# First gates' sigmoids behind attention's exponentials, early tiles for the third product's weights, and mLSTM heads gated one by one

## The chip, the cores and the metric

The kernel runs on one core of one Trainium2 chip. The metric is the device time of one execution in microseconds (us), lower being better.

## The reference

Two layers of a hybrid decoder on 512 tokens of width 1024, in float32. Each layer computes one wide projection of the normalised input, from it two branches, merges them by gates, and adds a squared-ReLU MLP:

```python
    z = h @ w_in
    q_a, k_a, v_a, q_m, k_m, v_m, o_m, if_m, gates = jnp.split(z, splits, axis=-1)
    ...
    att = sliding_window_attention(q_a, k_a, v_a, att_sinks)
    ...
    hm = mlstm_chunkwise(...)
    hm = rmsnorm(hm, m_head_norm.reshape(M_HEADS, M_V_DIM)).reshape(B, S, M_V_W)
    hm = hm * jax.nn.sigmoid(o_m)

    g_a, g_m = jnp.split(gates, 2, axis=-1)
    mixed = jax.nn.sigmoid(g_a) * (att @ w_att_branch) + jax.nn.sigmoid(g_m) * (hm @ w_m_branch)
    x = x + mixed @ w_out

    u = jax.nn.relu(rmsnorm(x, norm_ffn) @ w_ff1)
    return x + (u * u) @ w_ff2
```

Attention has 8 query heads of 64 in 2 key/value groups, a window of 128 tokens and a learned sink per head that enters the softmax's denominator. The mLSTM branch has 4 heads with values of 128; each head is normalised by itself before the output gate sigmoid(o_m).

## The kernel before

A layer is `mixer` and then `mlp`. The change lies in `mixer`, in the part after the attention's projections.

**Products.** A float32 operand is split into a high and a low part (`wh`, `wl` of a weight, L165 and L166; `split`, L175 and L176, of an activation: the high part is a copy on ACT, the low part a subtraction on DVE), and a product is three TensorE matmuls: high by high, low by high, high by low. A weight chunk is 128x512, loaded on SP's queue (L155); its product with all 512 tokens is 12 matmuls.

**The weave.** The work is issued by `weave(fill, side)`: `fill` is the list of product steps in their order on TensorE, `side` a list of (time, function) pairs that are put in between at their time, counted in chunks of 12 matmuls. A scheduler then orders the instructions of each engine, by priority and by when it expects them to be ready; `tc.high_priority()` lifts what is issued inside it, `tc.issue_after(x)` keeps what is issued inside it behind instruction x. An engine runs its own instructions strictly in the order so made. Tiles come from pools: activations 128x512 from 32 slots (`slot()`, named `a`), temporaries from 17 (`temp()`, named `t`), three PSUM banks (`aux`) for the side work and five (`mm`) for products. A tile that is asked for waits for its buffer's last reader.

The fill after the attention's projections: mLSTM queries and keys; gate A in two halves (`s0`, `s1`, whose results are the four tiles each of `g0` and `g1`); the attention branch product in two halves (`a_steps`), whose results are multiplied into `g0` and `g1` by `ev_a` (L909); seven products that give values and the output gate (`vo_steps`); gate B (`s2`, `s3`).

**Gates.** The evacuation `ev` (L699) multiplies a gate's product by the row norm into a slot; after the last of `g1`, `sigmoid` (L686) is issued for all eight tiles, and `back` (L692) loads the table of Exp and Ln again. Sigmoid lies in another table, so ACT_TABLE_LOAD rows appear around it. Copies run with either table.

**Attention.** Its eight units (b, kv), block b of 128 queries and group kv, are on the side list: scores (L587 to L601), softmax (row maximum L608, its combination with the sinks L609, the sink's term L611, four exponentials L614, the sink's exponential `es` L616, denominators L617 and L618, scaling L619), transposes into PSUM (L52 on TensorE) with a split into high and low (L175, L176) and a causal select of both on POOL (L634), and the output (four matmuls; L645 and L649 bring both halves together, L652 and L653 split the result into tiles `a` for the branch product). The last units are (3,0) and (3,1).

**Values and the output gate.** They come from 2x2 blocks by a scheme of seven products instead of eight, in the order 5, 1, 3, 6, 2, 7, 4. Their weights are sums of blocks of `w_in`: `load` (L714) copies a block on SP's queue, `more` (L718) adds another to it by an accumulating DMA on POOL's. `wa` serves products 5, 6 and 4, and is begun early by `begin` (L727); `wb` serves 3 and 7, and is loaded where product 3 first asks for it, in `weight` (L732). `parts_of` (L723, L724) splits such a weight; products 1 and 2 take plain blocks, as chunks of the ordinary kind. The activations' sums are `sums[n]`. `value` and `output` (L795, L797) evacuate into `vm` and `so`; `gates_o` takes the sigmoid of `so`.

**mLSTM heads.** `m_decay`, `m_weights` and `m_out` (L860 to L892) handle head h and block t; `m_out` leaves its result in `hm[t]`, columns of head h, and the sum of squares in `hss` (L892). `m_norm` (L895 to L901) makes the norms and, for each t, multiplies `hm[t]` by them (L900) and by `so[t]` (L901). `head_tr(f)` transposes head f of all four blocks (L52) for the mLSTM branch product.

Of the kernel before, what the change touches and what calls it, by code (L numbers as in the profile page):

```python
# [9 lines left out]
F32R = mybir.dt.float32r  # L10
# [23 lines left out]
def hybrid_kernel(ctx, tc, x, norm_mix, w_in, att_q_norm, att_k_norm, att_sinks, m_gate_bias,  # L34
# [27 lines left out]
    def nm(s):  # L62
        uid[0] += 1
        return f"{s}_{uid[0]}"
# [323 lines left out]
    def mixer(l, norm, late, order, phase):  # L388
# [152 lines left out]
            gp.tensor_tensor(xv[:, :, 0:ROPE], t1, t2, op=ALU.add)  # L541

        att_acts = [(slot(F32R), slot(F32R)) for _ in range(4)]
        qT, sps, parts = {}, {}, {}
        tri_i = tri_l.bitcast(I32)

        def k_vec(b):
# [55 lines left out]
        def att_softmax(b, kv):  # L603
            sp = sps[b, kv]
            s3 = sp.rearrange("p (h k) -> p h k", h=4)
            hs = slice(4 * kv, 4 * kv + 4)
            m = sm([P, 4], "m")
            ve.tensor_reduce(m, s3, axis=AX.X, op=ALU.max)  # L608
            ve.scalar_tensor_tensor(m, m, -1.0, nsinks[:, l, hs], op0=ALU.mult, op1=ALU.min)  # L609
            es = sm([P, 4], "es")  # L610
            ve.tensor_tensor(es, sinks[:, l, hs], m, op=ALU.add)  # L611
            den = sm([P, 4], "den")
            for i in range(4):
                sc.activation(s3[:, i, :], s3[:, i, :], AF.Exp, bias=m[:, i:i + 1],  # L614
                              accum_out=den[:, i:i + 1])
            sc.activation(es, es, AF.Exp)  # L616
            ve.tensor_tensor(den, den, es, op=ALU.add)  # L617
            ve.reciprocal(den, den)  # L618
            ve.tensor_tensor(s3, s3, den.unsqueeze(2).to_broadcast([P, 4, P]), op=ALU.mult)  # L619
# [90 lines left out]
            return W[(4 * i + k) * P:(4 * i + k + 1) * P, c0:c0 + T]  # L710

        def load(r, i, j, k):
            with tc.high_priority():
                nc.sync.dma_start(r, block(i, j, k))  # L714

        def more(r, i, j, k):
            with tc.high_priority():
# [9 lines left out]
        def begin(k):  # L727
            wa[k] = temp()
            load(wa[k], 0, 0, k)
            more(wa[k], 0, 1, k)  # L730

        def weight(n, k):  # L732
            if n in (1, 2):
                return chunk([block(n - 1, 0, k)])
            if n == 3:
                wb[k] = slot()
                load(wb[k], 1, 1, k)
            w = parts_of((wb if n in (3, 7) else wa)[k])
            if n == 5:
                more(wa[k], 1, 1, k)  # L740
            if n == 6:
                more(wa[k], 1, 0, k)
            if n == 3:
                more(wb[k], 0, 1, k)
            return w
# [2 lines left out]
            return [f32(g[:, :, H * t:H * (t + 1)]) for g in norm.groups[i]]  # L748

        def sum_parts(key, src):  # L750
            sums[key] = [split(src[:, 2 * p:2 * p + 2, :], get=lambda: now["tmp"].tile([P, 2, H], F32R, tag="t", name=nm("t")))
                         for p in range(2)]

        def sums1():
            a, b = (mid.tile([P, 4, H], F32, tag=t, name=nm("sc")) for t in ("mid6", "kvi"))
# [91 lines left out]
        side += [(8.45 + 3.0 * i, f) for i, f in enumerate((gating0, gating1, gating2, gating3))]  # L847
        side += [(9.6 + 1.65 * n, lambda n=n: qk_split(n // 2, n % 2)) for n in range(8)]
        g0, s0 = gate_steps(0)
        g1, s1 = gate_steps(1, lambda: back(sigmoid(g0 + g1)))  # L850

        hm = q_tok
        hss = sm([P, NB, MH], "hss", 1)
# [27 lines left out]
        def m_out(h, t):  # L881
            ps = aux([P, MV + 1])
            for s in range(t + 1):
                pe.matmul(ps, wts[h, s][:, (t - s) * P:(t - s + 1) * P], vm[0][:, s, h, :],
                          start=s == 0, stop=s == t)
            dn = sm([P, 1], "dn")
            ve.scalar_tensor_tensor(dn, ps[:, MV:], -1.0, em[:, t, h:h + 1], op0=ALU.mult, op1=ALU.max)
            ve.tensor_tensor(dn, ps[:, MV:], dn, op=ALU.max)
            ve.reciprocal(dn, dn)
            hs = hm[t][:, h * MV:(h + 1) * MV]  # L890
            sc.activation(hs, ps[:, :MV], AF.Copy, scale=dn)
            sc.activation(ps[:, :MV], hs, AF.Square, accum_out=hss[:, t, h:h + 1])  # L892

        def m_norm():
            ve.tensor_scalar(hss, hss, 1.0 / MV, EPS, op0=ALU.mult, op1=ALU.add)  # L895
            hr = sm([P, NB, MH], "hr", 1)
            rsqrt(hr, hss, "hq")
            for t in range(NB):
                h3 = hm[t].rearrange("p (h v) -> p h v", h=MH)
                ve.tensor_tensor(h3, h3, hr[:, t, :].unsqueeze(2).to_broadcast([P, MH, MV]), op=ALU.mult)  # L900
                ve.tensor_tensor(hm[t], hm[t], so[t], op=ALU.mult)  # L901

        prod = []

# [7 lines left out]
                              ev_a)  # L912

        side += [(25.0 + 0.5 * k, lambda k=k: begin(k)) for k in range(4)]
        side += [(25.0, sums1), (28.5, lambda: sums_next(6, 0, 0)), (31.5, lambda: sums_next(3, 0, 1)), (36.5, sums3)]
        pace = 3.2
        for h in range(MH):
            at = 39.6 + pace * h
            side.append((at, lambda h=h: m_decay(h)))
            for i in range(NB):  # L920
                side += [(at + 1.75 + pace * i / NB, lambda h=h, i=i: m_weights(h, i)),
                         (at + 4.65 + pace * i / NB, lambda h=h, i=i: m_out(h, i))]
        side.append((56.9, m_norm))
        g2, s2 = gate_steps(2)
        g3, s3 = gate_steps(3, lambda: back(sigmoid(g2 + g3)))
# [5 lines left out]
                pe.transpose(ps[:, b * P:(b + 1) * P], hm[b][:, f * P:(f + 1) * P], ident)  # L931
            hmT.append(split(ps, g_head(l, f)))

        side += [(58.4 + 1.0 * f, lambda f=f: head_tr(f)) for f in range(MH)]
        weave(feat_steps(acts, wcols(C_QM, 512), ev_qk) + s0 + s1 + a_steps(0, g0) + a_steps(1, g1) + vo_steps
              + s2 + s3, side)
        sgm = [g2, g3]
# [549 lines left out]
```

## Time and profile before

| | |
|---|---|
| median of 3 runs | 1325.09 us (1323.92 to 1325.39) |
| the profiled execution | 1325.29 us, of which its span is 1323.6 us |
| TensorE busy (PE) | 1290.8 us, 98% of the span, 6930 matmuls |
| VectorE busy (DVE) | 1011.8 us, 76% |
| ScalarE busy (ACT) | 798.0 us, 60% |
| GpSimd busy (POOL) | 227.9 us, 17% |

A line of a timeline gives the start in us from the span's start, the busy time, engine, source line, operation, output <- input tiles, shapes, and how many instructions were joined; in brackets stands the idle time of that engine before it and what ended that. PE is TensorE's matmuls, DVE VectorE, ACT ScalarE, POOL GpSimd, SP SyncE (DMA issues). PEclk is the clock that TensorE was granted, 1 being full speed. Line numbers are those of the kernel before.

### The profile page before, as it was taken

To read this page: it belongs to the slowest core of one execution; us is meant where nothing else is said; L and a number is where in the kernel's file an instruction comes from. 1 tells how busy PE (TensorE), PEld (TensorE's weight loads), DVE (VectorE), ACT (ScalarE), POOL (GpSimd) and SP (SyncE) were. 2 spreads that over 40 slices of the span, in tenths; PEclk is the share of its full clock that TensorE was granted. 3 is DMA by queue.
4 is the path that set the end of the run, shared out by engine and by line. 5 is a ranking of instruction groups with operands and counts; after the bars stand their busy time and mean duration, and the time that the engine had idled before them with its cause. 6 is when DMAs were issued, how large, how long until landed. Compare 5 with 4: busy or idle time off the path is not lost. (4 is left out here: it accounts for less than half of the span.)

```text
span 1323.6 us, 19221 instructions
## 1 busy us (share of the span) xinstructions
PE 1290.8 (98%) x6930; PEld 1097.9 (83%) x6930; DVE 1011.8 (76%) x1581; ACT 798.0 (60%) x1385; POOL 227.9 (17%) x313
## 2 busy tenths in 40 slices
PE   9999799999999999999999988999999999999998
PEld 7877677878889999999888766788888899999987
DVE  4699876576578897978958998665746778879697
ACT  5568568643565665656554784695534656666563
POOL 4511230000003121131115112210000030311310
PEclk9999899999999999999999998999999999999999
DMA  5422483263358989898124225822723698988953
GB/s 152 109 73 64 97 165 89 71 214 121 89 150 154 232 192 204 201 207 220 32 75 111 64 64 115 179 65 72 238 80 97 159 180 233 186 207 201 204 158 96
DMA packets 135150, 186.00 MB, mean 141 GB/s; under 512 B 10376, under 2 KB 78832, under 8 KB 135056
## 3 DMA queue, kind: packets, MB, share of 16 engines
q1 hardware_dynamic: 94208, 131.82, 32.3%
q0 software_dynamic: 40128, 52.57, 25.1%
q8 instruction: 54, 0.88, 0.3%
q10 hardware_dynamic: 720, 0.40, 0.1%
q14 instruction: 40, 0.33, 0.1%
HBM read 182.65 MB, written 2.10 MB: 140 GB/s over the span
## 5 line engine op out<-in xcount | busy, mean ns | idle before, releaser
L47 PE MATMUL mm<-i,wh 128*128 128x512 f32 (+1 forms) x1280 | 355.5, 363 | 0.0
L983 ACT ACTIVATE wh<-raw 128x1024 fp32r<-128x1024 f32 x212 | 223.0, 1055 | 187.4 <-PE mm L47 116.6
L984 DVE TENSOR_TENSOR wl<-raw,wh 128x1024 fp32r<-128x1024 f32 x212 | 255.4, 1221 | 75.0 <-ACT wh L983 75.0
L47 PEld LDWEIGHTS mm<-i,wh 128*128 128x128 f32 x1280 | 223.8, 189 | 31.0 <-DVE a L699 0.8
L47 PE MATMUL mm<-i,wl 128*128 128x512 f32 (+1 forms) x640 | 230.2, 360 | 0.0
L166 DVE TENSOR_TENSOR wl<-w,wh 128x512 fp32r<-128x512 f32 (+1 forms) x192 | 129.2, 676 | 106.9 <-ACT wh L165 103.9
L165 ACT ACTIVATE wh<-w 128x512 fp32r<-128x512 f32 (+1 forms) x192 | 116.9, 610 | 125.3 <-PE mm L47 94.2
L47 PE MATMUL mm<-wh,uh 128*128 128x512 f32 x440 | 171.8, 390 | 0.0
L47 PE MATMUL mm<-wl,uh 128*128 128x512 f32 x440 | 171.7, 390 | 0.0
L47 PE MATMUL mm<-wh,ul 128*128 128x512 f32 x440 | 171.2, 389 | 0.0
L1143 POOL DMA_DIRECT2D raw<-in_w_ff_dram x48 | 62.2, 1303 | 545.7 <-DMA raw<-in_w_ff_dram 370.1
L47 PEld LDWEIGHTS mm<-i,wl 128*128 128x128 f32 x640 | 120.8, 189 | 17.7 <-DVE wl L984 0.4
L47 PE MATMUL mm<-wh,i 128*128 128x512 f32 (+1 forms) x352 | 100.7, 360 | 2.6 <-ACT wh L165 2.3
L1029 DVE SCALAR_TENSOR_TENSOR x<-mm,ms,x 128x512 f32<-128x512 f32 x126 | 90.7, 745 | 9.2 <-PE mm L47 9.1
L47 PEld LDWEIGHTS mm<-wh,ul 128*128 128x128 f32 x440 | 82.6, 188 | 17.6
L47 PEld LDWEIGHTS mm<-wh,uh 128*128 128x128 f32 x440 | 82.8, 188 | 16.0
L47 PEld LDWEIGHTS mm<-wl,uh 128*128 128x128 f32 x440 | 82.8, 188 | 15.5
L47 PE MATMUL mm<-wh,a 128*128 128x512 f32 x256 | 81.8, 393 | 0.0
L47 PE MATMUL mm<-a,wh 128*128 128x512 f32 x256 | 79.3, 391 | 0.0
L47 PEld LDWEIGHTS mm<-wh,i 128*128 128x128 f32 x352 | 61.9, 188 | 14.2 <-ACT wh L165 3.3
L1300 POOL DMA_DIRECT2D raw<-in_w_ff_dram x36 | 44.1, 1224 | 149.4 <-DVE wl L984 100.9
L47 PE MATMUL aux<-i,wh 128*128 128x256 f32 x384 | 69.5, 283 | 0.0
(283 smaller groups left out, 2430.9 us busy)
## 6 DMA issues: line engine op xcount, KB each, us to landing
raw<-in_w_ff_dram SPq DMA_DIRECT2D x144, 512.0 KB, 5.2
raw<-in_w_ff_dram POOLq DMA_DIRECT2D x84, 512.0 KB, 8.0
w<-in_w_in_dram SPq DMA_DIRECT2D x112, 256.0 KB, 2.7
w<-in_w_out_dram SPq DMA_DIRECT2D x32, 256.0 KB, 2.8
t<-in_w_in_dram POOLq DMA_DIRECT2D x24, 256.0 KB, 6.2
w<-in_w_att_branch_dram SPq DMA_DIRECT2D x16, 256.0 KB, 2.6
w<-in_w_m_branch_dram SPq DMA_DIRECT2D x16, 256.0 KB, 2.7
w<-in_w_in_dram SPq DMA_DIRECT2D x16, 128.0 KB, 2.1
```

What stands on the lines that cost most here:

```text
L47: latest[0] = nc.tensor.matmul(*args, **kw)
L165: sc.activation(wh[:, :off], raw[:, :off], AF.Copy)
L166: ve.tensor_tensor(wl[:, :off], raw[:, :off], f32(wh[:, :off]), op=ALU.subtract)
L983: sc.activation(hi, src, AF.Copy)
L984: ve.tensor_tensor(lo, src, f32(hi), op=ALU.subtract)
L1029: ve.scalar_tensor_tensor(xh[:, cc], ps[i][:, cc], ms[j][:, b:b + 1], xh[:, cc], op0=ALU.mult, op1=ALU.add)
L1143: gp.dma_start(to[h], src(h, i, j), accum_op=ALU.add)
L1300: gp.dma_start(to[h], src(h, i, j), accum_op=ALU.add)
```

## The change

It has three parts. The eight sigmoids of `g0` and `g1` are issued behind `last_exp`, the `es` exponential of the last attention unit. The weights of product 3 get temporary tiles (`temp()`) and are loaded from the side list at 27.0 to 28.5 by `begin_other`, not in `weight`; the loads and the accumulation in `begin` lose their high priority, and the activation sums of product 3 get slots in place of temporaries. The output gate is multiplied into each head and block by `m_gate`, right behind `m_out` (for head 0 at 46.8 to 47.4), in place of the four multiplications in `m_norm`; the heads' transposes move from 58.4 + 1.0 f to 59.2 + 0.8 f.

```diff
--- before.py
+++ after.py
@@ -541,7 +541,7 @@
             gp.tensor_tensor(xv[:, :, 0:ROPE], t1, t2, op=ALU.add)
 
         att_acts = [(slot(F32R), slot(F32R)) for _ in range(4)]
-        qT, sps, parts = {}, {}, {}
+        qT, sps, parts, last_exp = {}, {}, {}, [None]
         tri_i = tri_l.bitcast(I32)
 
         def k_vec(b):
@@ -613,7 +613,7 @@
             for i in range(4):
                 sc.activation(s3[:, i, :], s3[:, i, :], AF.Exp, bias=m[:, i:i + 1],
                               accum_out=den[:, i:i + 1])
-            sc.activation(es, es, AF.Exp)
+            last_exp[0] = sc.activation(es, es, AF.Exp)
             ve.tensor_tensor(den, den, es, op=ALU.add)
             ve.reciprocal(den, den)
             ve.tensor_tensor(s3, s3, den.unsqueeze(2).to_broadcast([P, 4, P]), op=ALU.mult)
@@ -710,8 +710,7 @@
             return W[(4 * i + k) * P:(4 * i + k + 1) * P, c0:c0 + T]
 
         def load(r, i, j, k):
-            with tc.high_priority():
-                nc.sync.dma_start(r, block(i, j, k))
+            nc.sync.dma_start(r, block(i, j, k))
 
         def more(r, i, j, k):
             with tc.high_priority():
@@ -727,14 +726,15 @@
         def begin(k):
             wa[k] = temp()
             load(wa[k], 0, 0, k)
-            more(wa[k], 0, 1, k)
+            gp.dma_start(wa[k], block(0, 1, k), accum_op=ALU.add)
+
+        def begin_other(k):
+            wb[k] = temp()
+            load(wb[k], 1, 1, k)
 
         def weight(n, k):
             if n in (1, 2):
                 return chunk([block(n - 1, 0, k)])
-            if n == 3:
-                wb[k] = slot()
-                load(wb[k], 1, 1, k)
             w = parts_of((wb if n in (3, 7) else wa)[k])
             if n == 5:
                 more(wa[k], 1, 1, k)
@@ -748,8 +748,9 @@
             return [f32(g[:, :, H * t:H * (t + 1)]) for g in norm.groups[i]]
 
         def sum_parts(key, src):
-            sums[key] = [split(src[:, 2 * p:2 * p + 2, :], get=lambda: now["tmp"].tile([P, 2, H], F32R, tag="t", name=nm("t")))
-                         for p in range(2)]
+            get = ((lambda: slot(F32R, (P, 2, H))) if key == 3
+                   else lambda: now["tmp"].tile([P, 2, H], F32R, tag="t", name=nm("t")))
+            sums[key] = [split(src[:, 2 * p:2 * p + 2, :], get=get) for p in range(2)]
 
         def sums1():
             a, b = (mid.tile([P, 4, H], F32, tag=t, name=nm("sc")) for t in ("mid6", "kvi"))
@@ -847,7 +848,11 @@
         side += [(8.45 + 3.0 * i, f) for i, f in enumerate((gating0, gating1, gating2, gating3))]
         side += [(9.6 + 1.65 * n, lambda n=n: qk_split(n // 2, n % 2)) for n in range(8)]
         g0, s0 = gate_steps(0)
-        g1, s1 = gate_steps(1, lambda: back(sigmoid(g0 + g1)))
+        def gates_a():
+            with tc.issue_after(last_exp[0].ins):
+                back(sigmoid(g0 + g1))
+
+        g1, s1 = gate_steps(1, gates_a)
 
         hm = q_tok
         hss = sm([P, NB, MH], "hss", 1)
@@ -890,6 +895,12 @@
             hs = hm[t][:, h * MV:(h + 1) * MV]
             sc.activation(hs, ps[:, :MV], AF.Copy, scale=dn)
             sc.activation(ps[:, :MV], hs, AF.Square, accum_out=hss[:, t, h:h + 1])
+            if h:
+                m_gate(h, t)
+
+        def m_gate(h, t):
+            c = slice(h * MV, (h + 1) * MV)
+            ve.tensor_tensor(hm[t][:, c], hm[t][:, c], so[t][:, c], op=ALU.mult)
 
         def m_norm():
             ve.tensor_scalar(hss, hss, 1.0 / MV, EPS, op0=ALU.mult, op1=ALU.add)
@@ -898,7 +909,6 @@
             for t in range(NB):
                 h3 = hm[t].rearrange("p (h v) -> p h v", h=MH)
                 ve.tensor_tensor(h3, h3, hr[:, t, :].unsqueeze(2).to_broadcast([P, MH, MV]), op=ALU.mult)
-                ve.tensor_tensor(hm[t], hm[t], so[t], op=ALU.mult)
 
         prod = []
 
@@ -912,6 +922,7 @@
                               ev_a)
 
         side += [(25.0 + 0.5 * k, lambda k=k: begin(k)) for k in range(4)]
+        side += [(27.0 + 0.5 * k, lambda k=k: begin_other(k)) for k in range(4)]
         side += [(25.0, sums1), (28.5, lambda: sums_next(6, 0, 0)), (31.5, lambda: sums_next(3, 0, 1)), (36.5, sums3)]
         pace = 3.2
         for h in range(MH):
@@ -920,6 +931,7 @@
             for i in range(NB):
                 side += [(at + 1.75 + pace * i / NB, lambda h=h, i=i: m_weights(h, i)),
                          (at + 4.65 + pace * i / NB, lambda h=h, i=i: m_out(h, i))]
+        side += [(46.8 + 0.2 * t, lambda t=t: m_gate(0, t)) for t in range(NB)]
         side.append((56.9, m_norm))
         g2, s2 = gate_steps(2)
         g3, s3 = gate_steps(3, lambda: back(sigmoid(g2 + g3)))
@@ -931,7 +943,7 @@
                 pe.transpose(ps[:, b * P:(b + 1) * P], hm[b][:, f * P:(f + 1) * P], ident)
             hmT.append(split(ps, g_head(l, f)))
 
-        side += [(58.4 + 1.0 * f, lambda f=f: head_tr(f)) for f in range(MH)]
+        side += [(59.2 + 0.8 * f, lambda f=f: head_tr(f)) for f in range(MH)]
         weave(feat_steps(acts, wcols(C_QM, 512), ev_qk) + s0 + s1 + a_steps(0, g0) + a_steps(1, g1) + vo_steps
               + s2 + s3, side)
         sgm = [g2, g3]
```

On ACT, at the end of attention in layer 0, before: t_1454 holds the scores of unit (3,0), t_1555 those of (3,1), aux_1647 the transposes of (3,0), and a_1766 to a_1770 are tiles of `g1` (the tiles of `g0` had their sigmoids, between loads of their own, in the middle of attention):

```order
L686 ACTIVATE a_1766<-a_1766 128x512
L686 ACTIVATE a_1768<-a_1768 128x512
L686 ACTIVATE a_1770<-a_1770 128x512
L692 ACT_TABLE_LOAD
L614 ACTIVATE t_1454,den_1540<-t_1454,m_1535 128x128 x4
L616 ACTIVATE es_1538<-es_1538 128x4
L652 ACTIVATE a_628<-t_1594 128x128
L652 ACTIVATE a_630<-t_1594 128x128
L614 ACTIVATE t_1555,den_1626<-t_1555,m_1621 128x128 x4
L616 ACTIVATE es_1624<-es_1624 128x4
L175 ACTIVATE t_1652<-aux_1647 128x512
```

and now, where a_1400 to a_1406 are `g0` and a_1764 to a_1770 `g1`:

```order
L616 ACTIVATE es_1624<-es_1624 128x4
L686 ACT_TABLE_LOAD
L686 ACTIVATE a_1400<-a_1400 128x512
L686 ACTIVATE a_1402<-a_1402 128x512
L686 ACTIVATE a_1404<-a_1404 128x512
L686 ACTIVATE a_1406<-a_1406 128x512
L686 ACTIVATE a_1764<-a_1764 128x512
L686 ACTIVATE a_1766<-a_1766 128x512
L686 ACTIVATE a_1768<-a_1768 128x512
L686 ACTIVATE a_1770<-a_1770 128x512
L692 ACT_TABLE_LOAD
L175 ACTIVATE t_1652<-aux_1647 128x512
```

The exponentials of both units went ahead of the sigmoids, all eight of which now stand, with a table load on either side, ahead of the split of the transposes (L175).

On VectorE at the same place, before: L699 evacuates `g1`, and m_1535 and m_1621 are the row maxima of (3,0) and (3,1):

```order
L699 TENSOR_TENSOR a_1764<-mm_1408,t_473 128x512
L699 TENSOR_TENSOR a_1766<-mm_1421,t_473 128x512
L699 TENSOR_TENSOR a_1768<-mm_1446,t_473 128x512
L699 TENSOR_TENSOR a_1770<-mm_1450,t_473 128x512
L609 SCALAR_TENSOR_TENSOR m_1535<-m_1535,nsinks 128x4
L649 TENSOR_TENSOR t_1594<-aux_1588,t_1593 64x256
L611 TENSOR_TENSOR es_1538<-sinks,m_1535 128x4
L649 TENSOR_TENSOR t_1594<-aux_1588,t_1593 64x256
L166 TENSOR_TENSOR wl_1881<-w_1878,wh_1880 128x512
L601 COPY_PREDICATED t_1555<-tri_l,aux_1614 128x256
L608 TENSOR_REDUCE m_1621<-t_1555 128x4
L609 SCALAR_TENSOR_TENSOR m_1621<-m_1621,nsinks 128x4
```

and now:

```order
L609 SCALAR_TENSOR_TENSOR m_1535<-m_1535,nsinks 128x4
L611 TENSOR_TENSOR es_1538<-sinks,m_1535 128x4
L601 COPY_PREDICATED t_1555<-tri_l,aux_1614 128x256
L608 TENSOR_REDUCE m_1621<-t_1555 128x4
L609 SCALAR_TENSOR_TENSOR m_1621<-m_1621,nsinks 128x4
L166 TENSOR_TENSOR wl_1860<-w_1857,wh_1859 128x512
L699 TENSOR_TENSOR a_1764<-mm_1408,t_473 128x512
L699 TENSOR_TENSOR a_1766<-mm_1421,t_473 128x512
L699 TENSOR_TENSOR a_1768<-mm_1446,t_473 128x512
L699 TENSOR_TENSOR a_1770<-mm_1450,t_473 128x512
...
L653 TENSOR_TENSOR a_631<-t_1594,a_630 128x128
L611 TENSOR_TENSOR es_1624<-sinks,m_1621 128x4
```

The steps of both softmaxes ahead of their exponentials moved in front of the four evacuations, but for es_1624, the sink's term of (3,1), which now stands eight rows behind them (after L653).

On SP's queue, the loads (L155) of ordinary chunks and those (L714 before, L713 now) of the seven products' blocks, before, the last four being product 3's:

```order
L714 DMA t_1869<-in_w_in_dram 128x512
L155 DMA w_2066<-in_w_in_dram 128x512
L155 DMA w_2078<-in_w_in_dram 128x512
L155 DMA w_2090<-in_w_in_dram 128x512
L155 DMA w_2222<-in_w_in_dram 128x512
L155 DMA w_2234<-in_w_in_dram 128x512
L155 DMA w_2246<-in_w_in_dram 128x512
L714 DMA a_2106<-in_w_in_dram 128x512
L714 DMA a_2129<-in_w_in_dram 128x512
L714 DMA a_2142<-in_w_in_dram 128x512
L714 DMA a_2155<-in_w_in_dram 128x512
L155 DMA w_2269<-in_w_in_dram 128x512
```

and now, product 3's being t_1878, t_1892, t_1900 and t_1920:

```order
L713 DMA t_1878<-in_w_in_dram 128x512
L155 DMA w_2074<-in_w_in_dram 128x512
L713 DMA t_1892<-in_w_in_dram 128x512
L155 DMA w_2086<-in_w_in_dram 128x512
L713 DMA t_1900<-in_w_in_dram 128x512
L713 DMA t_1920<-in_w_in_dram 128x512
L155 DMA w_2098<-in_w_in_dram 128x512
L155 DMA w_2222<-in_w_in_dram 128x512
L155 DMA w_2234<-in_w_in_dram 128x512
L155 DMA w_2246<-in_w_in_dram 128x512
L155 DMA w_2269<-in_w_in_dram 128x512
```

They moved ahead of four or more chunk loads (w_2222, w_2234 and w_2246 are the same in both), and no longer ask for a slot.

## The prediction

> **What bounds the kernel now.** I read the page first, then TensorE's waits by releaser, then the timelines of PE, ACT and DVE around the longest of them, then the clock by window.
>
> ```profile
> span 1323.6 us, 19221 instructions
> ...
> PE 1290.8 (98%) x6930; PEld 1097.9 (83%) x6930; DVE 1011.8 (76%) x1581; ACT 798.0 (60%) x1385; POOL 227.9 (17%) x313
> ```
>
> TensorE is busy in 1290.8 of 1323.6 us, and the change neither adds nor removes a matmul. It can only move TensorE's idle 33 us and the clock at which its work runs. The waits list names the idle time by what ended it (total, times, longest):
>
> ```profile
> PE aux L52 <- DVE t L619: 13.9, 4, 6.7
> PE mm L47 <- ACT wh L723: 3.2, 2, 1.8
> PE mm L47 <- ACT wh L165: 2.3, 3, 0.9
> PE aux L52 <- DVE a L901: 1.8, 2, 0.9
> PE aux L47 <- ACT t L581: 1.5, 2, 0.7
> ...
> PE mm L47 <- DVE wl L166: 0.4, 2, 0.2
> ```
>
> The first row, seen in layer 0 and then in layer 1 on TensorE's timeline (start, duration, idle before in brackets):
>
> ```profile
> 142.77 1.09 PE L52 MATMUL aux<-ident,t 128*128 128x128 f32 x4 [6.68 <-DVE t L619]
> 143.51 2.06 PE L47 MATMUL aux<-t,v 128*128 128x512 f32 x4
> ...
> 150.38 1.36 PE L47 MATMUL mm<-a,wh 128*128 128x512 f32 x5
> ...
> 798.35 1.08 PE L52 MATMUL aux<-ident,t 128*128 128x128 f32 x4 [6.72 <-DVE t L619]
> ...
> 805.96 1.32 PE L47 MATMUL mm<-a,wh 128*128 128x512 f32 x5
> ```
>
> After the gate product TensorE has nothing but the last two attention units, (3,0) and (3,1), between itself and the attention branch product, which begins at 150.38. ACT's timeline shows why they are late:
>
> ```profile
> 134.38 1.28 ACT L686 ACT_TABLE_LOAD   x1
> ...
> 136.73 1.65 ACT L686 ACTIVATE a<-a 128x512 f32<-128x512 f32 x3
> 138.40 1.28 ACT L692 ACT_TABLE_LOAD   x1
> ...
> 143.28 0.19 ACT L616 ACTIVATE es<-es 128x4 f32<-128x4 f32 x1
> 143.89 0.60 ACT L175 ACTIVATE t<-aux 128x512 fp32r<-128x512 f32 x1 [0.42 <-PE aux L52]
> ```
>
> A table load, four sigmoids and a load back, 5.3 us from 134.38 to 139.68, stand ahead of the exponentials of (3,0). The idle time also costs clock: the column after the busy times is the granted one.
>
> ```profile
> 148.00:150.00 2.00, 1.59 (x7) 1.01 (x6) 1.75 (x4) 1.12 (x3) 1.44 (x2) 0.92 0.02 4
> 802.00:804.00 2.00, 2.00 (x6) 1.57 (x6) 1.96 (x5) 1.31 (x4) 1.19 (x2) 0.58 0.49 131
> ```
>
> A mean of 0.92 over 148 to 150 means half speed until 148.3 (0.32 us at 0.5, the rest at 1); likewise 0.58 gives 803.7. Full clock returned 5.5 and 5.3 us after TensorE did, so before the branch product.
>
> **Part 1, the first gates' sigmoids.** They leave their place ahead of the exponentials, and all eight of a layer stand, between two table loads, behind es (L616) of (3,1) and ahead of the split of P^T(3,0) (L175). So the transposes come earlier, but what they feed comes later. I date that split. VectorE now does five rows of (3,0) and (3,1) before the gates' quartet, and its one gap goes:
>
> ```profile
> 118.39 0.69 DVE L166 TENSOR_TENSOR wl<-w,wh 128x512 fp32r<-128x512 f32 x1 [0.98 <-ACT wh L165]
> 134.06 2.75 DVE L699 TENSOR_TENSOR a<-mm,t 128x512 f32<-128x512 f32 x4
> 136.73 0.15 DVE L609 SCALAR_TENSOR_TENSOR m<-m,nsinks 128x4 f32<-128x4 f32 x1
> 137.14 0.14 DVE L611 TENSOR_TENSOR es<-sinks,m 128x4 f32<-128x4 f32 x1
> 137.31 0.42 DVE L649 TENSOR_TENSOR t<-aux,t 64x256 f32<-64x256 f32 x1
> 137.76 0.69 DVE L166 TENSOR_TENSOR wl<-w,wh 128x512 fp32r<-128x512 f32 x1
> 138.37 0.43 DVE L601 COPY_PREDICATED t<-tri_l,aux 128x256 f32<-128x256 int32 x1
> 138.84 0.69 DVE L608 TENSOR_REDUCE m<-t 128x4 f32<-128x512 f32 x1
> 139.56 0.16 DVE L609 SCALAR_TENSOR_TENSOR m<-m,nsinks 128x4 f32<-128x4 f32 x1
> ```
>
> The five are 0.15 + 0.14 + 0.43 + 0.69 + 0.16 = 1.57; the quartet starts at 134.06 + 1.57 - 0.98 = 134.65. It cannot end before TensorE's last gate product at 136.1 plus one evacuation of 0.69, so an earlier start would win 0.5 at most. Behind it follow a weight split 0.69, two operations on the denominators (128x4 like L609, 0.16 each), two L649 at 0.42, L619 (128x512, as L166, 0.69), two L653 (128x128, 0.28 each, as the row of part 3) and L611 0.14; with the quartet's 2.75 that is 6.0, and as neighbours overlap by up to 0.08 I take 5.5: L611 done at 140.2. Then ACT: es 0.19, load 1.28, eight sigmoids at 1.65/3 = 0.55 or a little less (4.3), load 1.28, so the split begins at X = 147.2, against 143.89.
>
> From X to the branch product TensorE has out(3,0) and out(3,1), eight matmuls, and two small ones. The causal selects of (3,0) on POOL hold the first four until about X + 2.5 (split 0.6; two selects estimated, from the 128x512 passes on the other engines, at 0.7 each; the last matmul). Then six at the half-clock pitch of 2.06/4 less overlap, 0.44, end at X + 5.15. The product begins at 152.35 against 150.38: **+1.95 a layer**. The eight sigmoids taken from earlier places, and two table loads less, are ACT time that lies beside a TensorE with other work: nothing. The score groups that move up into the gate product are priced as a rival.
>
> The clock: TensorE idles from 136.2 to about 139.6, works on (3,0) and (3,1) until 142, idles to X + 0.6 = 147.8. If full speed returns 5.4 us after that, at 153.2, 0.9 us of the product run at half, +0.4. If the gap-ridden stretch does not count and the 5.4 start with the product, 157.7, it is +2.7. No row decides between them; I take the middle, +1.5. **Together +3.45 a layer, +6.9** (bounds +0.8 to +4.6 a layer: the low end has the quartet 0.5 earlier and the early 0.55 us waits of the score groups gone).
>
> In sentences apart: the Trainium skill, TensorE: Matmul & The Clock Gate, Part 1: The HAM clock gate, says the clock is halved after an idle window of about 3.4 us and restored after about 3.4 us of busy time. By it the clock would be back at 151.2, no product would run at half, and A would be +1.5 or so a layer. This trace's 5.5 and 5.3 do not agree with 3.4.
>
> **Part 2, product 3's weights.** Before, the slots for them came free late, and the four loads stood behind other weights on SP's queue:
>
> ```profile
> 185.35 0.73 PE L47 MATMUL mm<-wh,t 128*128 128x512 f32 x2 [1.75 <-ACT wh L723]
> 181.59 1.84 SPq L714 DMA_DIRECT2D a<-in_w_in_dram  x4
> 840.57 0.73 PE L47 MATMUL mm<-wh,t 128*128 128x512 f32 x2 [1.40 <-ACT wh L723]
> 201.94 0.50 PE L47 MATMUL mm<-wh,i 128*128 128x512 f32 x1 [0.78 <-ACT wh L165]
> 857.00 0.50 PE L47 MATMUL mm<-wh,i 128*128 128x512 f32 x1 [0.86 <-ACT wh L165]
> ```
>
> Now they are loaded some 30 us before use, into temporary tiles; nothing but ACT's split is left in front, and that has the weights ready. **-1.75 - 1.40 = -3.15.** Product 2's waits, 0.78 + 0.86 + 0.44 on wl = 2.08, come from one weight load that follows those four on SP and whose data runs beside eight accumulations on POOL. Four of these move early; half the wait goes: **-1.0** (0 to -2.1). Loads and accumulations without high priority could come later, but they are used far behind their issue: nothing, or product 1 waits for them up to the same 1.75 (taken into the range).
>
> **Part 3, head gates.** Four 128x512 multiplications between the norm and the transposes go; sixteen 128x128 come, and the transposes stand five matmuls later.
>
> ```profile
> 266.38 0.30 PE L52 MATMUL aux<-ident,a 128*128 128x128 f32 x1 [0.89 <-DVE a L901]
> 264.33 0.69 DVE L900 TENSOR_TENSOR a<-a,hr 128x512 f32<-128x512 f32 x1
> L879 DVE TENSOR_TENSOR t<-t,aux 128x128 f32<-128x128 f32 x8 | 2.3, 282 | 0.7 <-POOL t L873 0.4
> ```
>
> L900 four times and one weight split, 5 x 0.61, end at 267.4; TensorE comes to the transposes at 265.5 + 5 x 0.23 = 266.6 and now needs all four tiles at once, so it waits some 0.75 instead of 0.89: **-0.3** for both layers (-1.8 to +0.6). The gates are 16 x 0.28 = 4.5 us of VectorE a layer for 2.7 removed. Each waits for ACT's square of that head, and behind it on VectorE stand the weight split and the decay weights that TensorE reads next; they lie mostly in VectorE's idle time: **+0.6** (0 to +2).
>
> **Sum.** 6.9 - 3.15 - 1.0 - 0.3 + 0.6 = +3.05. The profiled execution took 1325.29, 0.2 above the median 1325.09; 1325.29 + 3.05 = 1328.34, on the median's scale 1328.1. A difference of 0.2% (2.65 us) is about what a measurement of this kernel can tell from none.
>
> **Rivals.** *A, faster: the attention end costs little and all weight waits go.* The quartet starts 0.5 earlier, the waits ahead of it go, the clock is back by the product: +0.8 a layer. With both of part 2's terms in full, 1.6 - 5.2 - 0.3 + 0.6 = -3.3: 1321.8. For it: every weight wait has a DMA behind it. Against: VectorE's queue ahead of L611 is full. *B, no change: the clock returns 3.4 us after TensorE*, as restated above; +1.5 a layer makes 3.0 - 3.85 = -0.85: 1324.2. Against it are both windows quoted. *C, much slower: the score groups moved up into the gate product stall TensorE.* They read rows that ACT and VectorE have just written; the row for L581 shows 0.74 us for such a wait. Two more of them in each layer, +3.0, on top of the forecast: 1331; with four, 1334. It decides once the scores are issued before the queries' transposes are copied. *D, the change does not do what it says:* the early loads still wait for a free temporary tile, and part 2 brings nothing while the sigmoids' new place is kept: 1332.
>
> The skill has one price that speaks for more: ScalarE: Activation LUTs, What ACT_TABLE_LOAD costs, gives a drain of about 1.38 us beside the load. With two drains in the new path, the sum would be about 1333.6. The quoted rows do not show it: the load back starts at 138.40, 0.02 after the sigmoids' end at 138.38.
>
> **How the numbers follow.** Forecast 0.48 (slower 0.38, within 0.2% 0.10: its own range is 1325 to 1332); A 0.22 (faster 0.20, same 0.02); B 0.15 (same 0.13, faster 0.02); C 0.09 and D 0.06, of D 0.03 the same. Faster 0.22, same 0.28, slower 0.50. The low end, 1319.5, is A with two waits more gone; the high end, 1334, is C with four stalls.
>
> **What would show it.** Right: the transposes that now wait 6.68 come near 139.6, and a second wait of about 5 us on L175 or its low part stands behind; two table loads fewer a layer; no row for L723; the branch product at 152.4, with a clock of 0.5 in its first microsecond. Wrong: the product starts by 150.4, or the wait behind the splits is under 4 us; new rows on the score groups; a wait on L903.

## The result, and the profile after

| kernel | median us | ratio to the kernel before, 95% interval |
|---|---|---|
| before (20 runs) | 1325.41 | |
| changed (20 runs) | 1326.02 | 1.0005 (0.9998 to 1.0012) |

The change makes no difference that this measurement can tell. Two large effects of opposite sign stand behind that. TensorE's waits in the changed kernel (total, times, longest; lines behind L712 have moved by up to 12):

```profile
PE aux L47 <- DVE t L176: 10.8, 2, 5.6
PE aux L52 <- DVE t L619: 7.2, 4, 3.4
...
PE aux L47 <- DVE t L884: 1.5, 4, 0.5
...
PE aux L47 <- DVE kT L561: 1.1, 2, 0.5
PE aux L47 <- DVE t L601: 1.0, 2, 0.5
PE aux L52 <- DVE t L649: 1.0, 4, 0.3
...
PE mm L47 <- ACT wh L165: 0.3, 1, 0.3
```

The 13.9 us on L619 became 7.2, and 10.8 on the low part of the split (L176) are new. The waits on product 3's split (3.2) are gone and those on product 2's (2.3) nearly so. ACT's timeline in layer 0 has the block in its new place:

```profile
140.10 0.20 ACT L616 ACTIVATE es<-es 128x4 f32<-128x4 f32 x1 [0.69 <-DVE es L611]
140.32 1.28 ACT L686 ACT_TABLE_LOAD   x1
141.62 4.27 ACT L686 ACTIVATE a<-a 128x512 f32<-128x512 f32 x8
145.90 1.28 ACT L692 ACT_TABLE_LOAD   x1
147.20 0.60 ACT L175 ACTIVATE t<-aux 128x512 fp32r<-128x512 f32 x1
```

TensorE's timeline, in layer 0 and layer 1, and the granted clock (the column behind the five busy times):

```profile
139.74 1.09 PE L52 MATMUL aux<-ident,t 128*128 128x128 f32 x4 [3.36 <-DVE t L619]
...
148.57 3.78 PE L47 MATMUL aux<-t,v 128*128 128x512 f32 x8 [5.19 <-DVE t L176]
...
152.81 1.08 PE L47 MATMUL mm<-a,wh 128*128 128x512 f32 x4
...
794.95 1.09 PE L52 MATMUL aux<-ident,t 128*128 128x128 f32 x4 [3.37 <-DVE t L619]
...
803.79 3.78 PE L47 MATMUL aux<-t,v 128*128 128x512 f32 x8 [5.57 <-DVE t L176]
...
808.10 1.09 PE L47 MATMUL mm<-a,wh 128*128 128x512 f32 x4
```

```profile
150.00:152.00 2.00, 2.00 (x6) 1.59 (x5) 1.48 (x5) 0.59 (x1) 1.51 (x2) 0.50 0.00 0
152.00:154.00 2.00, 2.00 (x9) 1.40 (x9) 1.82 (x5) 1.00 (x3) 0.00 (x0) 0.86 0.88 106
806.00:808.00 2.00, 2.00 (x6) 1.44 (x5) 1.30 (x4) 1.09 (x4) 0.78 (x1) 0.52 0.38 20
```

From the end of the gate product (the start of the transposes less the wait ahead of them) to the branch product it took 14.29 and 14.33 us before; now it takes 152.81 - 136.38 = 16.43 and 808.10 - 791.58 = 16.52. That is 2.14 and 2.19 longer. The product's first four matmuls take 1.08 us, full speed: the clock was back at 152.6 and 807.9, just ahead of it. These rows are those of one execution, which took 1324.49 us, 1.5 below the changed kernel's median; the profiled execution of the kernel before took 1325.29.

### The profile page after: what moved, and what is told of

Read it like the earlier page. It is cut to its first block, busy times and chain, and to the rows that moved or that the text cites. A ratio compares the mean times of both kernels' runs of the same rounds, so it can differ in the third digit from the quotient of the medians.

```text
span 1322.8 us, 19239 instructions
## 1 busy us (share of the span) xinstructions
PE 1290.1 (98%) x6930; PEld 1101.3 (83%) x6930; DVE 1012.6 (77%) x1605; ACT 794.8 (60%) x1381; POOL 228.7 (17%) x313
## 4 chain that ended last, share of the span: by engine, by line
PE 83%; DVE 6%; issue 5%; POOL 3%; ACT 2%; DMA 1%; DVEq 0%; POOLq 0%; SPq 0%; ACTq 0%
PE mm L47 66%; PE aux L47 14%; PE aux L52 2%; DVE wl L166 1%; DVE a L699 1%; ACT a L686 1%; DMA w<-in_w_in_dram 1%; POOL rp L536 1%; DVE t L582 0%; POOL rq L539 0%; POOL rq L537 0%; DVE t L601 0%; POOL t L878 0%; DVE t L649 0%; DVE t L619 0%
## 5 line engine op out<-in xcount | busy, mean ns | idle before, releaser
L165 ACT ACTIVATE wh<-w 128x512 fp32r<-128x512 f32 (+1 forms) x192 | 117.0, 610 | 115.3 <-PE mm L47 88.2
L1155 POOL DMA_DIRECT2D raw<-in_w_ff_dram x48 | 62.2, 1303 | 547.4 <-DMA raw<-in_w_ff_dram 265.6
L47 PE MATMUL mm<-wh,a 128*128 128x512 f32 x288 | 91.7, 393 | 0.0
L47 PE MATMUL aux<-t,wh 128*128 128x256 f32 x384 | 69.6, 283 | 0.0
```

The costliest lines, as they stand in the source:

```text
L47: latest[0] = nc.tensor.matmul(*args, **kw)
L165: sc.activation(wh[:, :off], raw[:, :off], AF.Copy)
L1155: gp.dma_start(to[h], src(h, i, j), accum_op=ALU.add)
```

## The experiments

**The parts by themselves.** Three kernels are the one before with one part of the diff each, a fourth has the second and third parts and not the first; no further edit.

> The kernel before with the first part alone (sigmoids behind the last exponential). Theory (the changed kernel's trace: the branch product starts 2.4 and 2.1 us later, at full clock): +4.5 us on the kernel before, transposes after a wait of 3.4, a second wait of 5.2 to 5.6 on the low part of the split, full clock back before the product. Rival 1 (the prediction as written): +6.9, the product's first microseconds at half clock. Rival 2 (the sigmoids' place is nearly free, and the other parts bring as little): within 1.5 us of before.

Measured: 1332.18, ratio 1.0052 (1.004 to 1.0065), that is +7.0.

> The kernel before with the second part alone (product 3's weights early). Theory: the two waits on product 3's split (1.75 and 1.40) go, and of product 2's 2.08 all but some 0.2 to 0.5: -4.8 us. Rival 1 (the prediction): -4.15, half of product 2's waits stay. Rival 2: the weights are hidden anyway, what is saved is waited for elsewhere in the seven products: between -1.5 and 0.

Measured: 1318.57, ratio 0.9954 (0.9942 to 0.9967), -6.6. Of the waits on weights in the products this is all that is left, and TensorE's busy time is 2.9 below the 1290.8 of before:

```profile
PE mm L47 <- DVE wl L166: 0.2, 1, 0.2
...
PE 1287.9 (98%) x6930; PEld 1099.0 (84%) x6930; DVE 1011.7 (77%) x1581; ACT 798.7 (61%) x1385; POOL 228.0 (17%) x313
```

> The kernel before with the third part alone (heads gated one by one). Theory: waits of the heads' transposes fall from 1.8 to 1.1, waits on the decay weights rise from 0.6 to about 1.5 since the gates stand ahead of them on VectorE: +0.2, between -0.5 and +1. Rival: the gates lie beside other work and the transposes no longer wait: -1.8.

Measured: 1325.04, ratio 0.9998 (0.9988 to 1.0007): nothing. The waits on the norm's last row fell from 1.8 to 1.1, those on the decay weights stayed at 0.6; the rise to 1.5 in the changed kernel is not the gates' doing alone (with the early weights alone they are 1.0).

> The changed kernel without its first part (sigmoids where they were; early weights and head gates kept). Theory (the three parts add: +7.0, -6.6, -0.1 alone): 1318.5 us, 7 below the kernel before, with the 6.7 us wait on L619 back and no wait on L722. Rival (the parts disturb one another, since the early weights' loads and the late sigmoids meet on ACT and SP's queue): above 1321 or below 1316.

Measured: 1319.0, ratio 0.9956 (0.9943 to 0.9968). The parts add: 7.0 - 6.6 - 0.1 = +0.3 against +0.6 for all three, and without the first one the rest keep their gain. All of the loss is the sigmoids' place, and nearly all of the gain is the early weights.

**What in that place costs.** First the row that the block on ACT waits for, es (L611, 0.16 us), is put ahead of the four evacuations on VectorE:

```diff
-            ve.tensor_tensor(es, sinks[:, l, hs], m, op=ALU.add)
+            with tc.high_priority():
+                ve.tensor_tensor(es, sinks[:, l, hs], m, op=ALU.add)
```

> The changed kernel with the sink's term of the softmax (L611, tiny) in high priority, so that on VectorE it stands ahead of the four evacuations L699 and not behind them. Theory (the block on ACT cannot start before es of the last unit, which waits for that row until 140.1 while the exponentials end at 137.7): the table load starts 2.3 us earlier, so does the split, and the branch product; 4.6 below the changed kernel, 1321.4. Rival (the block then waits for the last evacuation of g1, which ends at 137.3 in any case, or the half clock eats it): 1 to 2 us below.

Measured: 1322.62, ratio to before 0.9983 (0.9974 to 0.9991), 3.4 below the changed kernel where 4.6 were expected. In layer 0 TensorE comes back 1.7 earlier than at 148.57, and part of that goes to the clock: the product's first four matmuls now run at half speed, 1.89 us for 1.08. In layer 1 they take 1.14.

```profile
146.83 3.78 PE L47 MATMUL aux<-t,v 128*128 128x512 f32 x8 [3.55 <-DVE t L176]
...
151.26 1.89 PE L47 MATMUL mm<-a,wh 128*128 128x512 f32 x4
```

Then the block's length, with only four sigmoids in it:

```diff
-        g0, s0 = gate_steps(0)
+        g0, s0 = gate_steps(0, lambda: back(sigmoid(g0)))
...
-                back(sigmoid(g0 + g1))
+                back(sigmoid(g1))
```

> The changed kernel with only the four sigmoids of g1 behind the last exponential; those of g0 are issued, with table loads of their own, when g0 is done. Theory (each sigmoid ahead of the split costs its 0.53 us on the path to the branch product): the split begins 2.1 us earlier, the wait on its low part falls from 5.2 to about 3.1, the product starts 2.1 earlier in each layer: 1321.8, 4.2 below the changed kernel. Rival (what costs is the early part, the moved score groups and the second idle stretch with its half clock, not the block's length): within 1.5 of the changed kernel.

Measured: 1325.97, ratio to before 1.0011 (1.0002 to 1.002): no gain. The rival's range came, but the run does not test the length. With the sigmoids of g0 back in mid-attention the scheduler did the exponentials of (3,1) behind the split of (3,0), the shorter block began 2.9 us later than in the changed kernel, and the split of (3,1) came at 148.67 where it had come at 148.44. It shows the half clock, though: TensorE returned at 149.68, the clock at 156.0 (0.51 over the last window), and the product paid for it.

```profile
141.01 0.60 ACT L175 ACTIVATE t<-aux 128x512 fp32r<-128x512 f32 x1 [1.85 <-PE aux L52]
141.51 0.39 ACT L614 ACTIVATE t<-t,m 128x128 f32<-128x128 f32 x1
...
143.26 1.28 ACT L686 ACT_TABLE_LOAD   x1
...
148.67 0.60 ACT L175 ACTIVATE t<-aux 128x512 fp32r<-128x512 f32 x1
```

```profile
149.68 2.28 PE L47 MATMUL aux<-t,v 128*128 128x512 f32 x4 [2.37 <-DVE t L649]
...
152.26 2.07 PE L47 MATMUL mm<-a,wh 128*128 128x512 f32 x4
```

```profile
154.00:156.00 2.00, 2.00 (x6) 1.52 (x6) 1.97 (x5) 0.51 (x2) 0.00 (x0) 0.51 0.25 47
```

**What the half clock costs.** Spare matmuls, never read, keep TensorE at work through the wait:

```diff
-                pe.transpose(pt[:, i * P:(i + 1) * P], sp[:, i * P:(i + 1) * P], ident)
+                last_tr[0] = pe.transpose(pt[:, i * P:(i + 1) * P], sp[:, i * P:(i + 1) * P], ident)
...
             po = aux()
+            if (b, kv) == (NB - 1, 0):
+                with tc.issue_after(last_tr[0].ins):
+                    dummy = bank()
+                    for _ in range(14):
+                        pe.matmul(dummy, kTh[:, kv, 0:P], acts[0][0], start=True, stop=True)
```

> The changed kernel with 14 matmuls of 128x512 into a spare PSUM bank, never read, behind the transposes of unit (3,1), so that TensorE works through its wait on the split in each layer. Theory (the clock is halved in that stretch by the idle time, and the eight output matmuls run at half clock, 3.8 us instead of 2): full clock is back by 146, the output matmuls wait for POOL's selects only, the branch product starts near 151.8 instead of 152.8: 2 us below the changed kernel, 1324. Rival (the clock costs nothing there, the chain through POOL, ACT and VectorE sets the product's start): within 1 us of the changed kernel, or above it by what the 14 overrun the wait.

Measured: 1325.03, ratio 0.9997 (0.9989 to 1.0006). In layer 0 the 14 ended at 145.9, 3.1 us before the split's low part, and the output matmuls ran at half clock again (0.50 over 150 to 152). In layer 1 the wait left behind them was 1.75 us, and the clock was full (1.00) from 802 to 810:

```profile
804.92 2.22 PE L47 MATMUL aux<-t,v 128*128 128x512 f32 x7 [1.75 <-DVE t L176]
...
808.66 1.32 PE L47 MATMUL mm<-a,wh 128*128 128x512 f32 x5
```

From the first output matmul to the product this layer took 3.74 us at full clock; layer 0 of the same execution took 4.75 at half clock, and the changed kernel 4.24 and 4.31. So half clock costs this stage 0.5 to 1.0 us, as far as one execution shows. The time itself is inconclusive; so, with 24:

> As the kernel with 14 spare matmuls, but with 24 (5.5 us at full clock), since the 14 ended 3.1 us before the split came and the clock fell again. Theory (half clock costs the stretch from the split to the branch product 1 us a layer): granted clock 1.0 from 142 to 154, the eight output matmuls wait on POOL's selects only, product at 151.9 in layer 0: 2 us below the changed kernel, 1324.0. Rival (chain through POOL, ACT and VectorE, the clock is hidden behind it): clock 1.0 there and no gain, 1326; if the clock is at half when they start, they overrun by up to 5 us a layer and the time is above.

Measured: 1327.52, ratio 1.0021 (1.0011 to 1.0031).

```profile
142.14 6.86 PE L47 MATMUL mm<-i,kT 128*128 128x512 f32 x24
148.84 0.63 PE L47 MATMUL aux<-t,v 128*128 128x512 f32 x2
149.82 1.78 PE L47 MATMUL aux<-t,v 128*128 128x512 f32 x5 [0.34 <-POOL t L634]
...
153.16 1.33 PE L47 MATMUL mm<-a,wh 128*128 128x512 f32 x5
```

```profile
150.00:152.00 2.00, 1.91 (x7) 1.03 (x6) 1.50 (x3) 0.60 (x1) 2.00 (x4) 1.00 0.00 0
```

The clock is full, and from the first output matmul to the product it still takes 153.16 - 148.84 = 4.3 us, as at half clock (152.81 - 148.57 = 4.2): TensorE now waits for POOL's selects and the copies. That looks like the rival's reading, a half clock hidden behind POOL, but the 24 have also made POOL late. They read the keys' tile, whose buffer the tile `vm` takes over, so the memset of `vm` waits for them, and on POOL the selects stand behind it. The first two lines are from this kernel, the third is the first select of the changed one:

```profile
149.06 0.13 POOL L786 MEMSET vm<- 128x16 f32 x1 [16.37 <-PE mm L47]
149.12 2.51 POOL L634 TENSOR_SCALAR_AFFINE_SELECT t<-t 128x512 fp32r<-128x512 f32 x4
...
147.86 0.63 POOL L634 TENSOR_SCALAR_AFFINE_SELECT t<-t 128x512 fp32r<-128x512 f32 x1 [14.63 <-ACT t L175]
```

The selects began 1.26 us later than in the changed kernel, though the split had begun 0.18 earlier (147.02). So the run with 24 does not show that the half clock is hidden, and layer 1 with 14, where the memset was done at 803.4, ahead of the selects, speaks against it. How much of the excess over the changed kernel (1.5 us) is the overrun of the 24 is not shown.

**The sigmoids behind everything.**

```diff
-        g1, s1 = gate_steps(1, gates_a)
+        g1, s1 = gate_steps(1)
+        side.append((24.3, gates_a))
...
-            last_exp[0] = sc.activation(es, es, AF.Exp)
+            sc.activation(es, es, AF.Exp)
...
-                sc.activation(dh, b3[:, j, :], AF.Copy)
+                last_exp[0] = sc.activation(dh, b3[:, j, :], AF.Copy)
```

> The changed kernel with the eight sigmoids put behind the splits and output copies of the last attention unit (issued from the side list at 24.3) instead of behind its exponential; nothing else is changed. Theory (the price of part 1 is the place of 2 table loads and 8 sigmoids ahead of the split): the wait on the split's low part goes, the branch product starts near 146 instead of 152.8, some 7 us a layer: 1312 us, 14 below the changed kernel. Rival (the 7 us of ACT then stand ahead of the branch product's weight splits and of its evacuation, and PE waits there instead): 1318 to 1322, with a new wait on wh L165 or on L686 rows.

Measured: 1327.42, ratio 1.0018 (1.001 to 1.0027), above what either reading expected. At its own place the theory held, the product starts at 146.64 instead of 152.81; the gain was given back 26 us later, before product 5. The rival was right that it would be given back, and named the wrong place:

```profile
146.64 1.35 PE L47 MATMUL mm<-a,wh 128*128 128x512 f32 x5
...
172.85 0.80 PE L47 MATMUL mm<-wh,t 128*128 128x512 f32 x1 [3.54 <-DVE a L920]
```

```profile
154.68 5.11 SPq L155 DMA_DIRECT2D w<-in_w_in_dram  x3
159.84 2.32 SPq L713 DMA_DIRECT2D t<-in_w_in_dram  x5
```

```profile
170.84 0.63 ACT L722 ACTIVATE wh<-t 128x512 fp32r<-128x512 f32 x1 [6.15 <-DMA t<-in_w_in_dram]
```

The releaser L920 is only the last link: on VectorE it stands behind a weight split that waits for ACT, which waits 6.15 us for a DMA. On SP's queue, shown above, three block loads of product 5 stood behind three chunk loads (L155) that were waiting for raw buffers. The chunk loads of products 1 and 2 were then kept behind them:

```diff
             if n in (1, 2):
-                return chunk([block(n - 1, 0, k)])
+                with tc.issue_after(begun[0].ins):
+                    return chunk([block(n - 1, 0, k)])
...
-            load(wa[k], 0, 0, k)
+            begun[0] = load(wa[k], 0, 0, k)
```

(`load` now returns the instruction that it issues.)

> The kernel with the sigmoids behind the last unit's output copies, and the chunk loads of product 1 kept behind the first product's block loads on SP's queue. In the late-sigmoid kernel before it, three of those block loads stood behind chunk loads that waited for a raw buffer, issued at 159.8, and product 5 waited until 172.9. Theory (that queue alone gave the gain back): no wait on L920, the branch product still near 146.6, 6 us a layer below the changed kernel: 1314. Rival 1 (the weight splits on ACT, which the sigmoids hold up by 7 us, are the next limit): 1320 to 1324, new waits on wh L165. Rival 2 (the accumulations on POOL cannot be faster): no better than 1326.

Measured: 1323.07, ratio 0.9988 (0.9979 to 0.9997): 4.4 gained, 1314 was expected. Rival 1's time came, and its sign in part: the waits on wh L165 are 3.8 in total. The loads were issued at 151.8, but the weights still landed at 168, since the next queue was blocked in the same way. On POOL an accumulation for a later product (L717) waited until 160.39 for a split, with three of product 5's (L731) behind it:

```profile
160.39 0.87 POOL L717 DMA_DIRECT2D t<-in_w_in_dram  x1 [15.69 <-DVE wl L723]
160.94 2.98 POOL L731 DMA_DIRECT2D t<-in_w_in_dram  x3
```

```profile
168.03 0.63 ACT L722 ACTIVATE wh<-t 128x512 fp32r<-128x512 f32 x1 [8.67 <-DMA t<-in_w_in_dram]
```

The next edit puts product 5's accumulations first:

```diff
-            gp.dma_start(wa[k], block(0, 1, k), accum_op=ALU.add)
+            with tc.high_priority():
+                begun[1] = gp.dma_start(wa[k], block(0, 1, k), accum_op=ALU.add)
...
             if n == 5:
-                more(wa[k], 1, 1, k)
+                with tc.issue_after(begun[1].ins):
+                    gp.dma_start(wa[k], block(1, 1, k), accum_op=ALU.add)
```

> The late-sigmoid kernel with the chunk loads of product 1 behind the first product's block loads on SP's queue, and now also with the first product's four accumulations on POOL's queue ahead of those that follow it (in the kernel before it, three of them stood behind one that waited for a split until 160.4, and the weights landed at 168). Theory (two queues, each blocked at its head, gave the early branch product's gain back): no wait on the evacuation before product 5, another 3 us below 1323: 1320 or less. Rival (weight loads themselves, begun when the temporary tiles come free at 151.8, are the limit, or product 2's chunk loads, wh L165, are): 1322 to 1324, waits on wh L165 of 4 us or more.

Measured: 1314.5, ratio 0.9911 (0.9898 to 0.9925), and no wait before product 5 on the list. That is 8.6 gained where 3 were expected; the waits on wh L165, too, fell to 0.7. Last, the softmax's rows on VectorE were let in between the four evacuations:

```diff
-            ve.tensor_tensor(den, den, es, op=ALU.add)
-            ve.reciprocal(den, den)
-            ve.tensor_tensor(s3, s3, den.unsqueeze(2).to_broadcast([P, 4, P]), op=ALU.mult)
+            with tc.high_priority():
+                ve.tensor_tensor(den, den, es, op=ALU.add)
+                ve.reciprocal(den, den)
+                ve.tensor_tensor(s3, s3, den.unsqueeze(2).to_broadcast([P, 4, P]), op=ALU.mult)
```

(and the line of es, as above).

> The fastest kernel so far (late sigmoids, both queues mended) with the softmax's denominators, scaling and sink's term in high priority, so that on VectorE they stand between the evacuations L699 and not behind all four. Theory (the 3.4 us wait on L619 that is left in each layer is those four evacuations ahead of it): the wait falls to about 1.5, the half clock behind it goes too, 2 to 3 us a layer: 1309 to 1311. Rival (the weights of product 5 are then awaited, as they come at the same time as before): 1313 to 1315, a wait before product 5.

Measured: 1309.87, ratio 0.9886 (0.9872 to 0.99), the fastest, 15 us below the kernel before. The granted clock is 1.00 from 130 to 162 and from 786 to 818, so neither layer has half clock there. The 7.4 on L619 became

```profile
PE aux L52 <- DVE t L621: 3.7, 4, 1.5
PE aux L52 <- DVE t L651: 2.3, 2, 1.2
```

## Why the prediction was right or wrong

The range, 14.5 us wide, held the time; the likeliest case, +3, did not come, and the time lies in what the forecast left to "no change". Step by step:

- **The date of the split held.** X was put at 147.2 and is 147.20; L611 at 140.2 ends at 140.07; the transposes were put near 139.6 and start at 139.74. The product was put at 152.35 and starts at 152.81. The term +1.95 a layer measured +2.14 and +2.19.
- **The clock term, +1.5 a layer, failed: in the profiled execution it is 0.** The step that failed is the middle between "5.4 us after TensorE's second return" and "5.4 us after the product's start". Full clock came about 4.0 and 4.1 us after the second return, ahead of the product. The forecast took 5.5 and 5.3 for a delay that begins with TensorE's return; the same trace gives another reading. Before, the clock fell at 138.08 and 796.84 (0.52 in the first row below, 0.71 over 796 to 798) and came back at 148.32 and 803.68: half clock lasted 10.24 and 6.84 us, 3 and 2 times 3.41. The other rows below are the changed kernel's and go with those from 152 and 806 on shown above: there half clock lasted 13.64 us in layer 0, 4 times 3.41, and in layer 1 came 3.4 us of half clock, 3.4 of full and 6.8 of half:

```profile
138.00:140.00 2.00, 0.00 (x0) 0.00 (x0) 1.81 (x5) 1.97 (x3) 0.00 (x0) 0.52 0.20 60
...
138.00:140.00 2.00, 0.27 (x2) 0.30 (x3) 1.94 (x8) 0.51 (x2) 0.00 (x0) 0.73 0.39 127
...
794.00:796.00 2.00, 1.05 (x5) 1.08 (x6) 1.63 (x8) 1.17 (x4) 0.00 (x0) 0.57 0.43 131
796.00:798.00 2.00, 2.00 (x9) 1.49 (x7) 0.66 (x1) 1.99 (x4) 0.00 (x0) 0.58 0.00 0
...
800.00:802.00 2.00, 0.00 (x0) 0.00 (x0) 0.00 (x0) 1.98 (x4) 0.00 (x0) 0.78 0.01 2
```

So the delay after a return depends on where the return falls between two such moments, and no such moment can be had from the return alone. In the changed kernel the product met full clock by 0.2 us in both layers, in the kernel with part 1 alone by 0.3 (back at 152.3 and 811.0, products from 152.58 and 811.33), and with the earlier es it missed it in layer 0; other executions may differ. The Trainium skill, TensorE: Matmul & The Clock Gate, Part 1: The HAM clock gate, has about 3.4 us for this return; the forecast set that aside on two windows of one trace, and rival B, built on it, was nearer for this term. The same section calls the activity window free-running, and that agrees with the multiples of 3.41 us.
- **Left out of the sum: the score groups that move up.** Rival C had them as 3 us or nothing, and new rows on the score groups were named as a sign of being wrong; they came. Together with the neighbouring waits they cost 1.7 in the changed kernel: the rows of kT (1.1), L601 (1.0 for 0.3 before) and L649 on transposes (1.0) stand where 1.1 on wh L165 had stood (the two rows of before are below). With 4.3 for the product's start that is 6.0; the sigmoids' place alone measured +7.0 (+5.3 to +8.6). The forecast had 6.9 for it: the right size, by luck, with one wrong term and one missing. Some 1.0 of the 7.0 is in no row named here.

```profile
PE aux L52 <- ACT wh L165: 1.1, 2, 0.6
...
PE aux L52 <- DVE t L601: 0.3, 2, 0.2
```

- **Part 2 was mis-sized: -4.15 was forecast, -6.6 measured (-4.4 to -7.7).** Product 3's waits went as put, 3.15. Product 2's were halved in the sum and went but for 0.2. Those two make 5.0; the rest was in no idle row: TensorE's busy time fell by 2.9. Of that, 2.5 lies in the stretches of the seven products (172 to 305 and 822 to 846 before), where the granted clock is 1.00 with and without the early weights; that short waits for weights are counted there as busy is the likely reason, not a shown one.
- **Part 3:** +0.3 was forecast and nothing measured.
- **The sum, again.** By the parts as they measured alone it is 7.0 - 6.6 - 0.1 = +0.3, where the forecast had 6.9 - 4.15 + 0.3 = +3.05; all three together measured +0.6. So nearly all of the miss of 2.75 is part 2 (2.45), and the rest part 3 (0.4, less 0.1 at part 1). Inside part 1, 3.0 of clock that did not come stand against 1.7 for the score groups, 0.4 more on the start and the 1.0 without a row. No run had each of these alone, and the two profiled executions differ by -0.8 and not by +0.6, so this split of the small terms stays an account of the rows and not a proof.
- **The table loads' drain.** The quoted load back starts at 145.90, 0.01 after the sigmoids' end, and the split 0.02 after the load. The extra 1.38 us of ScalarE: Activation LUTs, What ACT_TABLE_LOAD costs, in the Trainium skill, does not show here either.

## What to carry to other kernels

Moving a block out of one wait puts it ahead of the next instruction of that engine: ask what now stands behind it, and date that from the engines' queues, which here hit the split and the product within half a microsecond. A gain made early on the path is kept only if what the path meets next was ready early too; look for loads and accumulations that stand behind a blocked head on a DMA queue. Price a late weight by its idle rows as a lower bound (5.2 us here, of 6.6 gained). Spare work put in to keep an engine busy can hold a buffer that another engine waits for: look at what its tiles keep from others before reading the result.

## What the runs showed of the hardware

In these two stretches the granted clock changed at moments that lie 3.41 us or a multiple of it apart: half clock lasted 10.24 and 6.84 us before, 13.64, 3.4 and 6.8 in the changed kernel, 17.1 in layer 0 with four sigmoids behind the last exponential (138.88 to 155.96). Full clock came back between 2.7 us (changed kernel, layer 1, 794.95 to 797.68) and 6.3 us after TensorE resumed, so the same return can fall before or behind a product's start: with the changed kernel its first four matmuls took 1.08 us, with the earlier es 1.89 in layer 0, though they began 1.5 us sooner. Idle stretches of 3.4 us were followed by half clock in some profiles and not in others: transposes after one took 1.09 us in the changed kernel, where the clock fell at 138.9, within the wait, and 0.63 in that with the late sigmoids, where it fell at 141.2 (0.79 over 140 to 142):

```profile
139.75 0.63 PE L52 MATMUL aux<-ident,t 128*128 128x128 f32 x4 [3.36 <-DVE t L619]
```
